# One hybrid decoder layer on one core: sample attention in 42 joined steps, forget rows a pair ahead, key pages in 2-KB runs, and three smaller edits

## The chip, the core and the metric

The kernel runs on one core of a Trainium2 chip. A core has five engines that each run their own queue of instructions in order: TensorE (PE, matrix products), VectorE (DVE), ScalarE (ACT), GpSimd (POOL) and SyncE (SP, which here only issues transfers and loads registers), and 16 DMA engines that carry the transfers which SP and ACT issue. Engines wait for one another by semaphores. The metric is the device time of one execution in microseconds; lower is better.

## The reference

One step of a decoder layer with three mixers side by side, in float32, for 1024 prompt tokens and for 8 samples of 8 new tokens each, all with the same weights:

```python
hn = rmsnorm(x, norm_pre)
u_a, z_a, q, k, v, f_lin, z_b, z_c, xbc, dt_raw, gates = split_cols(hn @ w_in)
y_a = pool_mixer(u_a) * silu(z_a)                        # A
o_b = fox_prompt(q, k, v, logf) or fox_sample(q, k, v, logf, past pages of k, v, logf)
y_b = o_b * silu(z_b)                                    # B
y_c = gated_group_rmsnorm(ssd_scan(conv(xbc), dt), z_c)  # C
g = sigmoid(gates)
m = g[0] * (y_a @ w_branch_a) + g[1] * (y_b @ w_branch_b) + g[2] * (y_c @ w_branch_c)
out = x + rmsnorm(m @ w_out, norm_post)
```

For a sample, attention runs over 1024 past positions, which lie in 8 pages of 128 positions (8 heads x 64) that a page table names, and over the 8 new ones. A logit is the product of query and key plus the difference of cumulated log-forget terms.

## The kernel before, in words

The 1088 tokens (NT) stand in columns, cut into chunks of 384, 384 and 320. Products need float32 accuracy, so each is done as three products of rounded operands: a matrix is split into a high part (`wh`, `hh`, `yh`, `ch`, `woh`, a cast on ACT) and the rest (`wl`, `hl`, `yl`, `cl`, `wol`, a subtraction on DVE or POOL), and `mm3` multiplies high by high, high by low and low by high.

The stages, in order: the projections and mixers A, B (prompt) and C; then the sample stage; then the A and B branches; the C branch; the output projection. The gate projections (`g<-hh,wh` and so on, from `gate_steps`) need only `hn`, so they are cut into steps and laid between the steps of other stages: `interleave(main, n_main, side, n_side, lag)` takes a step of the main work, then as many gate steps as are due by count; the lag keeps gate work from being scheduled earlier than the main step so many steps back.

The sample stage (`samples`, lines 896 to 1040) goes through four pairs m of samples. `load_k` and `load_v` bring pages by SP: it loads a page number into a register (`TENSOR_LOAD`, `ptab`), then issues the transfer of 256 KB (`kr<-ck`, two pages to a tile; `vr<-cv`, one). `scores(m)` fills three PSUM tiles s0, s1, s2 with products of the queries (`QB`, 32 columns at a time) with the K tiles and the new keys (`ksm`). `softmax(m)` loads the row of forget terms (`ck<-ckqD`), and on line 962 a DVE reduction adds it to the scores and takes the running minimum; exponentials (`T`) and normalisation follow. `values(m)` transposes the probabilities on PE (`pa<-cst,T`, `pa<-cst,Pn`), multiplies them by V pages (`po<-vr,PT`, `po<-vsm,PTn`) and stores the rows `ysm` that become the sample part of `ybD`. All PSUM tiles of this stage come from one pool of 5 buffers.

In the A/B stage (lines 1066 to 1100) the rows `yaD`, `ybD` come back by SP into a ring `fs` of three and are split into `yh` and `yl`; then for each of eight output rows 72 matmuls (`g<-yh,wh`), whose results DVE multiplies by gates that SP loads from `gD` into a ring `st` of five (`ld`); rows `ycD` are loaded, scaled and split into `ch`, `cl` between them. The C stage (lines 1101 to 1111) does the same with `ch`, `cl`. The output projection (from line 1113) loads `wo` in 16 halves into tiles `woh`, `wol` that lie over `ch`, `cl`.

## Time and profile before

| | |
|---|---|
| time, median of 3 runs | 1424.1 us (1422.5 to 1424.3) |
| the profiled execution | 1424.75 us, its span 1423.0 us |
| PE busy | 1374.1 us, 97% of the span |
| DVE, ACT, POOL busy | 47%, 36%, 31% |
| granted TensorE clock, mean | 0.992 of full speed |
| moved by DMA | 213.80 MB, 150 GB/s over the span |

The span is the time from the first to the last instruction of that execution. Busy times of different engines overlap. A matmul's row lasts longer than the distance to the next one, since matmuls are pipelined; what one costs is read from start to start. The clock has two levels, 1.2 and 2.4 GHz; a share below 1.00 in a stretch says that part of the stretch ran at the lower one.

### The profile page before, as it was taken

To read this page: it belongs to the slowest core of one execution; us is meant where nothing else is said; L and a number is where in the kernel's file an instruction comes from. 1 tells how busy PE (TensorE), PEld (TensorE's weight loads), DVE (VectorE), ACT (ScalarE), POOL (GpSimd) and SP (SyncE) were. 2 spreads that over 40 slices of the span, in tenths; PEclk is the share of its full clock that TensorE was granted. 3 is DMA by queue.
4 is the path that set the end of the run, shared out by engine and by line. 5 is a ranking of instruction groups with operands and counts; after the bars stand their busy time and mean duration, and the time that the engine had idled before them with its cause. 6 is when DMAs were issued, how large, how long until landed. Compare 5 with 4: busy or idle time off the path is not lost.

```text
span 1423.0 us, 23680 instructions
## 1 busy us (share of the span) xinstructions
PE 1374.1 (97%) x8936; PEld 1277.4 (90%) x8936; DVE 671.5 (47%) x1315; ACT 514.4 (36%) x1108; POOL 435.9 (31%) x383
## 2 busy tenths in 40 slices
PE   6999999999999999999999999998999999999997
PEld 5989999999999999998799898776789989999786
DVE  7493448536725833765963863110111663333423
ACT  6221255345534534546535642121123321122311
POOL 3124322222222222223644544111111353454300
PEclk9999999999999999999999999999899999999999
DMA  6124311411321241138675755988765985532421
GB/s 216 52 75 128 110 54 62 144 60 47 108 82 54 77 129 54 46 116 275 198 237 183 228 191 179 279 255 264 228 231 189 299 293 186 170 123 76 159 86 66
DMA packets 145471, 213.80 MB, mean 150 GB/s; under 512 B 20604, under 2 KB 78926, under 8 KB 145358
## 3 DMA queue, kind: packets, MB, share of 16 engines
q1 hardware_dynamic: 116878, 151.21, 33.4%
q10 hardware_dynamic: 28224, 60.83, 13.0%
q8 instruction: 70, 1.15, 0.3%
q0 software_dynamic: 256, 0.26, 0.1%
q14 instruction: 43, 0.35, 0.1%
HBM read 159.79 MB, written 54.58 MB: 151 GB/s over the span
## 4 chain that ended last, share of the span: by engine, by line
PE 82%; DMA 6%; DVE 6%; issue 2%; SPq 2%; ACT 1%; POOL 1%; DVEq 0%; ACTq 0%; POOLq 0%
PE g L71 60%; PE o L71 7%; PE po L71 4%; PE pa L71 4%; PE pa L75 3%; DMA kr<-ck 1%; PE pi L71 1%; DMA E<-cuD 1%; PE ph L71 1%; PE py L71 1%; PE s L71 1%; DMA fs<-ycD 1%; DVE win L449 1%; SPq L100 1%; DMA ybD<-o 1%
## 5 line engine op out<-in xcount | busy, mean ns | idle before, releaser
L71 PE MATMUL g<-hh,wh 128*128 128x384 f32 (+1 forms) x1632 | 545.9, 336 | 2.4 <-DVE z L237 1.5
L71 PE MATMUL g<-hh,wl 128*128 128x384 f32 (+1 forms) x1632 | 539.3, 331 | 0.0
L71 PE MATMUL g<-hl,wh 128*128 128x384 f32 (+1 forms) x1632 | 536.8, 329 | 0.3 <-DVE hl L303 0.3
L177 POOL TENSOR_TENSOR wl<-raw,wh 128x512 fp32r<-128x512 f32 x168 | 233.5, 1391 | 592.2 <-ACT wh L176 447.8
L71 PEld LDWEIGHTS g<-hh,wh 128*128 128x128 f32 x1632 | 308.1, 189 | 21.6 <-issue 14.3
L71 PEld LDWEIGHTS g<-hl,wh 128*128 128x128 f32 x1632 | 308.3, 189 | 4.9 <-issue 2.1
L71 PEld LDWEIGHTS g<-hh,wl 128*128 128x128 f32 x1632 | 308.0, 189 | 3.6 <-issue 1.6
L176 ACT CAST wh<-raw 128x512 fp32r<-128x512 f32 x168 | 103.9, 619 | 341.6 <-PE g L71 318.0
L599 POOL TENSOR_TENSOR ckd<-ckb,cst 128x128 f32<-128x128 f32 x64 | 33.3, 527 | 118.3 <-DVE mn L613 98.9
L71 PE MATMUL g<-yh,wh 128*128 128x384 f32 (+1 forms) x192 | 63.8, 332 | 5.0 <-DVE ld L1088 5.0
L249 ACT ACTIVATE gt<-g 128x384 f32<-128x384 f32 (+1 forms) x72 | 33.6, 470 | 88.1 <-PE g L71 63.2
L639 ACT CAST Ph<-pa 128x512 fp32r<-128x512 f32 (+1 forms) x96 | 44.7, 480 | 56.2 <-PE pa L75 51.9
L640 DVE TENSOR_TENSOR Pl<-pa,Ph 128x512 fp32r<-128x512 f32 (+1 forms) x96 | 51.3, 553 | 26.7 <-ACT Ph L639 20.2
L71 PE MATMUL g<-yh,wl 128*128 128x384 f32 (+1 forms) x192 | 63.6, 331 | 0.0
L71 PE MATMUL g<-yl,wh 128*128 128x384 f32 (+1 forms) x192 | 63.5, 331 | 0.0
L71 PE MATMUL g<-ch,wl 128*128 128x384 f32 (+1 forms) x192 | 62.7, 327 | 0.0
L71 PE MATMUL g<-cl,wh 128*128 128x384 f32 (+1 forms) x192 | 62.6, 326 | 0.0
L71 PE MATMUL g<-ch,wh 128*128 128x384 f32 (+1 forms) x192 | 62.6, 326 | 0.0
L617 ACT ACTIVATE T<-T,mn 128x128 f32<-128x128 f32 (+3 forms) x64 | 49.7, 777 | 30.8 <-DVE mn L613 30.8
L718 ACT ACTIVATE E<-E,cumN 128x128 f32<-128x128 f32 (+1 forms) x144 | 43.5, 383 | 37.9 <-DMA E<-cuD 31.3
L75 PE MATMUL pa<-cst,T 128*128 128x128 f32 x320 | 53.1, 272 | 0.0
L71 PE MATMUL o<-wol,mh 128*128 128x512 f32 x128 | 50.1, 399 | 0.9 <-DVE wol L1123 0.9
(266 smaller groups left out, 2057.6 us busy)
## 6 DMA issues: line engine op xcount, KB each, us to landing
raw<-w ACTq DMA_DIRECT2D x164, 256.0 KB
kr<-ck SPq DMA_DIRECT2D x64, 256.0 KB
vr<-cv SPq DMA_DIRECT2D x64, 256.0 KB
gD<-gt ACTq DMA_DIRECT2D x24, 544.0 KB
ld<-gD SPq DMA_DIRECT2D x24, 544.0 KB
E<-cuD SPq DMA_DIRECT2D x16, 512.0 KB
mD<-ld SPq DMA_DIRECT2D x8, 544.0 KB
fs<-mD SPq DMA_DIRECT2D x8, 544.0 KB
```

What stands on the lines that cost most here:

```text
L71: last["pe"] = nc.tensor.matmul(**kw)
L75: last["pe"] = nc.tensor.transpose(*args)
L100: recent.append(SP.dma_start(out=out, in_=in_))
L176: S.copy(wh, raw)
L177: G.tensor_tensor(wl, raw, wh.bitcast(F), op=SUB)
L249: S.activation(gt[:, a:b], ps, AF.Tanh, scale=0.5)
L449: V.tensor_tensor(dst[:, 2 * w - 1:W], src[:, 2 * w - 1:W], src[:, w - 1:W - w], op=ADD)
L599: G.tensor_tensor(ckd, ckb[e][:, i * 128:n], cst[:, C_M30:C_M30 + 128], op=ADD)
L617: S.activation(T[:, 0:n], T[:, 0:n], AF.Exp, scale=-1.0, bias=cur, accum_out=l[:, e, i:i + 1])
L639: S.copy(Ph[:, q0:512], ps[:, q0:512])
L640: V.tensor_tensor(Pl[:, q0:512], ps[:, q0:512], Ph[:, q0:512].bitcast(F), op=SUB)
L718: S.activation(E[0:nt, h, 0:nt], E[0:nt, h, 0:nt], AF.Relu, scale=-1.0, bias=cumN[0:nt, c, r0 + h:r0 + h + 1])
```

## The change

1. `samples` has 42 steps instead of 92: a scores step is now a K tile of each sample of the pair, a values step four V pages instead of two, and several steps of different kinds are taken together; the last step of a pair's values is taken with the first of the next pair's (`late`). The lag is 12 steps instead of 30.
2. The load of the forget row `ck` and the addition to its last columns stand at the start of `scores(m)` instead of at that of `softmax(m)`.
3. A K tile is laid out by page, so that a page's transfer writes 2 KB in one run to each partition instead of four runs of 512 B; the score products read two runs of 128 columns. The rings hold 8 K tiles and 10 V pages instead of 6 and 8; 6 K tiles and 8 V pages are asked for ahead instead of 5 and 7.
4. For odd rows k POOL computes `yl` instead of DVE.
5. `wo`'s first k-tile has two tiles of its own, `wo0h` and `wo0l`, from the ring `st`, loaded ahead of the C stage. The products of that k-tile for the first two row blocks are written ahead of the rest.

```diff
@@ -23 +23 @@
-LAG = (99, 99, 40, 30)
+LAG = (99, 99, 40, 12)
@@ -899,2 +899,2 @@
-        ak = px.enter_context(tc.tile_pool(name="ak", bufs=6))
-        av = px.enter_context(tc.tile_pool(name="av", bufs=8))
+        ak = px.enter_context(tc.tile_pool(name="ak", bufs=8))
+        av = px.enter_context(tc.tile_pool(name="av", bufs=10))
@@ -916 +916 @@
-                        kr = ak.tile([128, 4, 256], F, tag="kr", name="kr")
+                        kr = ak.tile([128, 2, 4, 128], F, tag="kr", name="kr")
@@ -918 +918 @@
-                            page_dma(out=kr[:, :, p * 128:p * 128 + 128],
+                            page_dma(out=kr[:, p],
@@ -920 +920 @@
-                        kraw.append(kr)
+                        kraw.append(kr.rearrange("p u c s -> p c u s"))
@@ -934 +934,5 @@
-            pss = score[m] = [psa(f"s{n}") for n in range(3)]
+            ck = a2.tile([128, 1032], F, tag="ck", name="ck")
+            SP.dma_start(out=ck, in_=ckqD[16 * m:16 * m + 16].rearrange("r q s -> (r q) s"))
+            V.tensor_tensor(ck[:, 1024:1032], ck[:, 1024:1032], cst[:, C_CA8:C_CA8 + 8], op=ADD)
+            pss = [psa(f"s{n}") for n in range(3)]
+            score[m] = pss, ck
@@ -944 +947,0 @@
-            yield
@@ -948,2 +951,2 @@
-                    products(pss[u // 2][:, u % 2 * 256:u % 2 * 256 + 256], bb, kraw.pop(0))
-                    yield
+                    products(pss[u // 2][:, u % 2 * 256:u % 2 * 256 + 256].rearrange("p (u s) -> p u s", u=2), bb, kraw.pop(0))
+                yield
@@ -953,4 +956 @@
-            pss, pn = score.pop(m), Pn[m % 2]
-            ck = a2.tile([128, 1032], F, tag="ck", name="ck")
-            SP.dma_start(out=ck, in_=ckqD[16 * m:16 * m + 16].rearrange("r q s -> (r q) s"))
-            V.tensor_tensor(ck[:, 1024:1032], ck[:, 1024:1032], cst[:, C_CA8:C_CA8 + 8], op=ADD)
+            (pss, ck), pn = score.pop(m), Pn[m % 2]
@@ -1005 +1005 @@
-                    if p % 2:
+                    if p % 4 == 3:
@@ -1027 +1027 @@
-            for _ in range(7):
+            for _ in range(8):
@@ -1029,0 +1030 @@
+            late = iter(())
@@ -1034,2 +1035,2 @@
-                for x in (s, v, s, v, s, v, k, v, k, v, k, v, k, v, k, v, k, v, k, v, k, v, k, v):
-                    if next(x, "end") != "end":
+                for x in ((s, late, v), (s,), (s,), (v, k), (v, k), (v, k), (v, k), (v,)):
+                    if [1 for g in x if next(g, "end") != "end"]:
@@ -1036,0 +1038,3 @@
+                late = v
+            next(late)
+            yield
@@ -1042 +1046 @@
-        for _ in range(5):
+        for _ in range(6):
@@ -1044 +1048 @@
-        interleave(samples(), 92, gate_steps(SHARE[2]), 6 * SHARE[2], LAG[3])
+        interleave(samples(), 42, gate_steps(SHARE[2]), 6 * SHARE[2], LAG[3])
@@ -1071 +1075 @@
-        V.tensor_tensor(yl[:, k], t, yh[:, k].bitcast(F), op=SUB)
+        (G if k % 2 else V).tensor_tensor(yl[:, k], t, yh[:, k].bitcast(F), op=SUB)
@@ -1100,0 +1105,13 @@
+    def load_wo(k, wh, wl):
+
+        for n in range(2):
+            sl = slice(n * 512, n * 512 + 512)
+            raw = wr.tile([128, 512], F, tag="raw", name="raw")
+            SP.dma_start(out=raw, in_=d["wo"][k, :, sl])
+            S.copy(wh[:, sl], raw)
+            (G if n else V).tensor_tensor(wl[:, sl], raw, wh[:, sl].bitcast(F), op=SUB)
+
+
+    wo = [[stq.tile([128, 1024], R, tag="st", name=x) for x in ("wo0h", "wo0l")]]
+    load_wo(0, *wo[0])
+
@@ -1118,7 +1135,3 @@
-    for k in range(8):
-        for n in range(2):
-            raw = wr.tile([128, 512], F, tag="raw", name="raw")
-            SP.dma_start(out=raw, in_=d["wo"][k, :, n * 512:n * 512 + 512])
-            S.copy(wh[:, k, n * 512:n * 512 + 512], raw)
-            (G if n else V).tensor_tensor(wl[:, k, n * 512:n * 512 + 512], raw,
-                                          wh[:, k, n * 512:n * 512 + 512].bitcast(F), op=SUB)
+    for k in range(1, 8):
+        wo.append([wh[:, k], wl[:, k]])
+        load_wo(k, *wo[k])
@@ -1129,0 +1143,15 @@
+    def out_mm(po, i, n, ks):
+        sl, tt = slice(n * 512, n * 512 + 512), slice(i * 128, i * 128 + 128)
+        for k in ks:
+            wh, wl = (x[:, sl] for x in wo[k])
+            if i < 8:
+                mm3(po, mh[:, k, tt], ml[:, k, tt], wh, wl, k == 0, k == 7)
+            else:
+                two = [(128, wh), (64, wl)]
+                for m_, x in two if k < 7 else two[::-1]:
+                    PE.matmul(out=po[0:m_], lhsT=mt[k // 4][:, k % 4, 0:m_], rhs=x,
+                              start=(k == 0 and m_ == 128), stop=(k == 7 and m_ == 128))
+
+    begun = {(i, n): psa(f"o{n}") for i in range(2) for n in range(2)}
+    for (i, n), po in begun.items():
+        out_mm(po, i, n, [0])
@@ -1140,9 +1168,5 @@
-            po = psa(f"o{n}")
-            for k in range(8):
-                if i < 8:
-                    mm3(po, mh[:, k, tt], ml[:, k, tt], wh[:, k, sl], wl[:, k, sl], k == 0, k == 7)
-                else:
-                    two = [(128, wh), (64, wl)]
-                    for m_, x in two if k < 7 else two[::-1]:
-                        PE.matmul(out=po[0:m_], lhsT=mt[k // 4][:, k % 4, 0:m_], rhs=x[:, k, sl],
-                                  start=(k == 0 and m_ == 128), stop=(k == 7 and m_ == 128))
+            po = begun.pop((i, n), None)
+            if po is None:
+                po = psa(f"o{n}")
+                out_mm(po, i, n, [0])
+            out_mm(po, i, n, range(1, 8))
```

What the change moves in the order of instructions is shown at three places. First SP, where it issues the rows `ck`. Before, the third of the four rows in the program (`ck_11178`, for the third pair; `ptab` is the page table, `ISA` an arithmetic instruction on registers):

```order
L100 DMA kr_11125<-ck 128x4x128
L955 DMA ck_11178<-ckqD_154 128x1032
L97 TENSOR_LOAD ptab_84
L97 ISA x2
L100 ISA
L100 DMA vr_11230<-cv 128x512
```

Now the third row:

```order
L97 TENSOR_LOAD ptab_84
L97 ISA x2
L935 DMA ck_10655<-ckqD_154 128x1032
L100 ISA
L100 DMA vr_10625<-cv 128x512
```

and the first two, with the first K page (`rst` is a small tile of the C mixer, `rsD1` where it is stored):

```order
L812 DMA ycD1_142<-gch_9399 512x1x64
L935 DMA ck_9698<-ckqD_154 128x1032
L848 DMA rsD1_160<-rst_9440 9x128
L935 DMA ck_10181<-ckqD_154 128x1032
L100 ISA
L100 DMA kr_9572<-ck 128x512
```

The third row stood right behind a run of K pages, with V pages after it; now 54 pages stand ahead of it, 44 of K and 10 of V. The rows of the first and the second pair stand ahead of all pages, with the store of `rst` between them.

PE, before, where the first value products come (`po<-vr,PT`):

```order
L71 MATMUL g<-hl,wh 128x384
L71 MATMUL g<-hh,wl 128x384
L75 MATMUL pa<-cst,Pn_9477 128x128
L71 MATMUL g<-hh,wh 128x384
L71 MATMUL g<-hl,wh 128x384
L71 MATMUL g<-hh,wl 128x384
L71 MATMUL po<-vr,PT 32x128 x8
L71 MATMUL g<-hh,wh 128x320
```

and now:

```order
L71 MATMUL g<-hh,wl 128x384
L71 MATMUL g<-hh,wh 128x384
L71 MATMUL g<-hl,wh 128x384
L71 MATMUL g<-hh,wl 128x384
L71 MATMUL po<-vr,PT 32x128 x16
L71 MATMUL s_10660<-ksm,QB 32x8 x8
L71 MATMUL s_10658<-kr,QB 32x256 x8
```

A values step has twice as many products, and the products of new keys and of two K tiles of a later pair (`s_10660`, `s_10658`) stand right behind it without gate matmuls between. Over the whole stage, from the first `ksm` product to the first matmul with `yh`, 58 runs of gate matmuls, 896 in all, become 36 runs with the same 896.

POOL at the end of the sample stage, before:

```order
L177 TENSOR_TENSOR wl_12599<-raw_12596,wh_12598 128x512
L177 TENSOR_TENSOR wl_12605<-raw_12602,wh_12604 128x512
L177 TENSOR_TENSOR wl_12691<-raw_12688,wh_12690 128x512
L177 TENSOR_TENSOR wl_12697<-raw_12694,wh_12696 128x512
L177 TENSOR_TENSOR wl_12830<-raw_12827,wh_12829 128x512
L177 TENSOR_TENSOR wl_12836<-raw_12833,wh_12835 128x512
```

and now:

```order
L177 TENSOR_TENSOR wl_12605<-raw_12602,wh_12604 128x512
L1075 TENSOR_TENSOR yl_12783<-fs_12788,yh_12782 128x1088
L177 TENSOR_TENSOR wl_12691<-raw_12688,wh_12690 128x512
L1075 TENSOR_TENSOR yl_12783<-fs_12796,yh_12782 128x1088
L177 TENSOR_TENSOR wl_12697<-raw_12694,wh_12696 128x512
L1075 TENSOR_TENSOR yl_12783<-fs_12804,yh_12782 128x1088
L177 TENSOR_TENSOR wl_12830<-raw_12827,wh_12829 128x512
L1075 TENSOR_TENSOR yl_12783<-fs_12812,yh_12782 128x1088
L177 TENSOR_TENSOR wl_12836<-raw_12833,wh_12835 128x512
```

The four `yl` subtractions of odd rows now stand between the weight splits `wl`, the last (from `fs_12812`) is behind `wl_12830`. On PE 168 gate matmuls instead of 156 stand between the last transposes of the sample stage and the first matmul with `yh`, and the output projection begins with 15 products of `wo0h` and `wo0l`.

## Rows read from the trace of the kernel before

**Rows 1.** The page's first part: busy time of each engine, its share of the span, and instructions.

```profile
PE 1374.1 (97%) x8936; PEld 1277.4 (90%) x8936; DVE 671.5 (47%) x1315; ACT 514.4 (36%) x1108; POOL 435.9 (31%) x383
```

**Rows 2.** Busy time of each engine in stretches of 100 us. Columns: stretch, its length, then busy us with the number of instructions for PE, weight loads, DVE, ACT and POOL, then the granted TensorE clock, the busy share of the DMA engines and GB/s.

```profile
900.00:1000.00 100.00, 85.55 (x742) 70.01 (x743) 9.76 (x32) 16.32 (x32) 12.38 (x10) 0.95 0.83 260
1000.00:1100.00 100.00, 100.00 (x975) 87.81 (x975) 12.59 (x38) 24.44 (x46) 15.61 (x12) 0.98 0.66 216
1100.00:1200.00 100.00, 95.00 (x562) 93.93 (x562) 54.10 (x67) 25.72 (x35) 43.60 (x26) 0.98 0.82 269
```

**Rows 3.** The list of waits of PE over the whole span. Columns: engine and line that waited, what it waited for, us in total, times, longest.

```profile
PE pa L75 <- DVE mn L962: 10.2, 1, 10.2
PE g L71 <- DVE ld L1088: 5.0, 3, 1.9
PE s L71 <- DMA kr<-ck: 4.3, 3, 2.7
```

**Rows 4.** The timeline around the longest of these waits, in this order: PE's transpose of `Pn` into `pa`, DVE's addition to the row `ck` ahead of its reductions, and SP's issues of six K pages and of the `ck` load. Columns: start, duration, engine and line (q: issued by the engine's queue), operation, out<-in, shape, count, and in brackets the idle time before it and what ended it.

```profile
999.41 0.47 PE L75 MATMUL pa<-cst,Pn 128*128 128x128 f32 x1 [10.20 <-DVE mn L962]
...
998.48 0.17 DVE L956 TENSOR_TENSOR ck<-ck,cst 128x8 f32<-128x8 f32 x1 [15.41 <-DMA ck<-ckqD]
...
984.76 8.20 SPq L100 DMA_DIRECT2D kr<-ck  x6
993.06 0.56 SPq L955 DMA_DIRECT2D ck<-ckqD  x1
```

**Rows 5.** Stretches of 10 us, columns as in rows 2; the third column from the end is the granted clock, as a share of full speed.

```profile
900.00:910.00 10.00, 7.32 (x75) 5.55 (x79) 0.78 (x3) 0.98 (x2) 0.83 (x1) 1.00 0.65 214
910.00:920.00 10.00, 9.81 (x72) 8.08 (x73) 2.28 (x8) 2.09 (x4) 1.29 (x1) 0.83 1.05 298
...
1000.00:1010.00 10.00, 10.00 (x92) 8.87 (x95) 3.06 (x10) 3.38 (x7) 1.27 (x1) 0.80 0.39 112
...
1310.00:1320.00 10.00, 8.42 (x41) 7.29 (x40) 6.44 (x7) 4.12 (x9) 6.21 (x5) 0.90 0.08 27
1320.00:1330.00 10.00, 10.00 (x41) 7.96 (x41) 3.19 (x5) 4.34 (x8) 3.40 (x3) 0.93 0.64 211
```

**Rows 6.** PE's timeline at the first K products of the sample stage. `s<-kr,QB` are score products, four instructions (eight records) for a K tile of two pages.

```profile
899.99 2.37 PE L71 MATMUL s<-kr,QB 128*32 128x256 f32 x40
902.28 0.44 PE L71 MATMUL g<-hl,wh 128*128 128x384 f32 x1
...
909.93 0.64 PE L71 MATMUL s<-kr,QB 128*32 128x256 f32 x8 [2.68 <-DMA kr<-ck]
910.50 0.41 PE L71 MATMUL g<-hh,wh 128*128 128x320 f32 x1
```

**Rows 7.** PE's timeline where value products `po` alternate with a run of twelve gate matmuls: a product, the first, second and last matmul of the run, the next product.

```profile
1080.68 0.65 PE L71 MATMUL po<-vr,PT 128*32 128x128 f32 x16
1081.26 0.44 PE L71 MATMUL g<-hh,wh 128*128 128x384 f32 x1
1081.54 0.34 PE L71 MATMUL g<-hl,wh 128*128 128x384 f32 x1
...
1083.28 0.34 PE L71 MATMUL g<-hh,wl 128*128 128x384 f32 x1
1083.54 0.64 PE L71 MATMUL po<-vr,PT 128*32 128x128 f32 x16
```

**Rows 8.** The page stream. First the instructions that issue K and V pages (line, engine, operation, tile, count, shortest/median/longest duration in ns, first and last start); then the page queue in two stretches, 930 to 947 (mostly K pages) and 1060 to 1080 (V pages): packets, MB moved, share of the 16 DMA engines' time; then SP's first K issues, the copy into `rst` on ACT, and SP's store of `rst`.

```profile
L100 SPq DMA_DIRECT2D kr<-ck x64: 542/544/2028, 885.2 to 1021.7; - x64
...
L100 SPq DMA_DIRECT2D vr<-cv x64: 332/333/1379, 918.5 to 1081.4; - x64
...
q1 hardware_dynamic: 6296, 3.13, 64.2%
...
q1 hardware_dynamic: 1619, 2.93, 42.8%
...
885.17 10.72 SPq L100 DMA_DIRECT2D kr<-ck  x12
...
895.66 0.25 ACT L847 COPY rst<-pa 9x128 f32<-9x128 f32 x1 [1.98 <-DMA kr<-ck]
...
899.44 0.35 SPq L848 DMA_DIRECT2D rsD<-rst  x1
```

**Rows 9.** The end of the sample stage: the first matmul with `yh`, the first three `yl` subtractions and the last on DVE, SP's issue of `gD` loads, and the first matmul of PE that waits for one. Last, the subtractions of the same size that POOL does in this stage (count, shortest/median/longest ns).

```profile
1117.47 0.34 PE L71 MATMUL g<-yh,wh 128*128 128x384 f32 x1
...
1097.27 3.70 DVE L1071 TENSOR_TENSOR yl<-fs,yh 128x1088 fp32r<-128x1088 f32 x3 [4.30 <-ACT yh L1070]
1114.59 1.29 DVE L1071 TENSOR_TENSOR yl<-fs,yh 128x1088 fp32r<-128x1088 f32 x1 [2.86 <-ACT yh L1070]
...
1117.64 1.85 SPq L1063 DMA_DIRECT2D ld<-gD  x4
...
1125.48 0.44 PE L71 MATMUL g<-yh,wh 128*128 128x384 f32 x1 [1.92 <-DVE ld L1088]
...
L1099 POOL TENSOR_TENSOR cl<-fs,ch x4: 2539/2748/3615, 1122.8 to 1159.1; 128x1088 fp32r<-128x1088 f32 x4
```

**Rows 10.** PE's timeline at the start of the output projection.

```profile
1315.65 0.49 PE L71 MATMUL o<-woh,mh 128*128 128x512 f32 x1 [0.71 <-ACT woh L1122]
1317.02 0.50 PE L71 MATMUL o<-wol,mh 128*128 128x512 f32 x1 [0.87 <-DVE wol L1123]
```

## The prediction

> **What bounds the kernel now.** I read the busy times first, then TensorE (PE) by windows of 100 us, then its list of waits, then the timeline around each wait. PE is busy for 1374.1 us of the span [rows 1]: it sets the end, and an edit pays only if it shortens PE's own work, removes a PE wait, or gives PE its clock back. The windows show where there is something to remove: 14.5 us idle in 900 to 1000 and 5.0 in 1100 to 1200 [rows 2]; 1000 to 1100 is full. The list of waits names them: one of 10.2 us behind a VectorE (DVE) reduction of line 962, three for K pages (4.3 us), three of 5.0 us in the A/B branch stage [rows 3]; two at the start of the output projection make 1.6 us [rows 10].
>
> The long one can be followed back. At 999.41 the transpose into `pa` got its PSUM buffer. It waited for a reduction of line 962, which needs the row `ck`; DVE had idled 15.41 us for it until 998.48; and SyncE (SP) issued that load at 993.06, behind six K pages whose issues, each with its register load, took 984.76 to 992.96 [rows 4]. So the load was late in SP's order, not slow.
>
> An idle PE also loses clock. In 910 to 920, after a K wait, the granted clock is 0.83; in 1000 to 1010 it is 0.80; in 1310 to 1330 it is 0.90 and 0.93 [rows 5]. Ten us at 0.83 instead of 1.00 are 1.7 us of lost work; so the dips cost 1.7, 2.0 and 1.7 us beside the waits.
>
> **The change part by part.**
>
> *Joined steps.* Counted in PE's program order from the first `ksm` product to the first `gy` matmul, 58 runs of gate matmuls become 36, with the same 896 gate matmuls and the same products. What does a switch cost? Ten steps inside a run take 1.74 us, 0.174 each; from the last gate to the product 0.26, and from the first gate after it to the second 0.28 [rows 7]: 0.19 us above 0.174 twice over, so about 0.20 per switch pair. Splitting K products costs a little more: 40 records take 2.29 us (0.057 each, 0.46 for 8), eight alone 0.57 [rows 6]. So 0.20 to 0.31 per pair; 22 fewer give -4.4 to -6.8. I take **-6**.
>
> *The `ck` row a pair ahead.* In the new order of SP the third row's load stands behind 54 pages: at 0.97 us a page from 897 (both below) it is issued at 949 and there by 955, as it took 5.4 us in before (993.06 to 998.48). PE reaches the transposes whose buffer hangs on its reductions at about 972, after V page 15 (964, below) and 36 more gate matmuls. The 10.2 us go, and the dip after them: 10.2 + 2.0 = **-12.2**. At 1.15 us a page the row comes at 964, still ahead; so I exclude that much of it stays.
>
> *K pages of 2-KB runs, two more ahead, wider rings.* K waits of 4.3 us and the dip of 1.7 can go: -6.0. What does a page cost? SP spends 0.544 us issuing a K page and 0.333 a V page, which already has 2-KB runs; in 930 to 947, mostly K pages, the queue moved 3.13 MB in 64.2% of 17 us, 287 GB/s; in 1060 to 1080, V pages, 2.93 MB in 42.8% of 20 us, 342 GB/s [rows 8]. A page is 262 KB: 0.91 and 0.77 us. With about a fifth of the DMA engines on the other queue (an estimate from both windows) that is 1.15 and 0.97 us per page.
>
> But the stream starts later and PE comes sooner. In before twelve K pages were issued from 885.17. Now the wider K ring lies over `rst`, so the first page must wait until the store `rsD<-rst` lands. That store was issued at 899.44; its source was copied at 895.66, after an idle time for a K page's DMA lane that is not yet in use now [rows 8]. I put the first page at 897 (894 to 900). PE needs few pages early: the new order has 33 gate matmuls ahead of the first K tile where before had five tiles at once at 899.99. The tight place is V pages 12 to 15, the 61st to 64th page transfers. PE gets there after 272 gate matmuls (by 0.165, mixed widths: 45), 22 K tiles (10), 12 V pages (3.4), small products and transposes (2.5) and 18 switches (3.6): 899.6 + 64.5 = 964. The pages get there at 897 + 64 x 0.97 + 2.5 for the row and the landing = 961.6, or, were a page no cheaper than before, at 973. So a new wait of 0 to 9 us, with a dip of up to 2. Nearest are the V rows, whose layout the K pages now have: **+1.5** (0 to +11).
>
> By the Trainium skill (DMA: Bandwidth & Descriptors, Specifications) a transfer is at line rate from 512 B up, so runs of 512 B would have nothing to gain; by that rule the wait would be the 9 us and the dip. The trace does not agree: 287 against 342 GB/s at equal engine share.
>
> *`yl` of odd rows on GpSimd (POOL).* The rows pass through a ring of three: row 4 is loaded when the `yl` of row 1 is done, row 7 after that of row 4; when the last has released its buffer, SP goes on to the `ycD` rows and then, from 1117.64, to four `gD` loads, on whose first arrival PE waits until 1125.48, 1.92 us [rows 9]. The first three `yl` take 3.70 us on DVE, the last one 1.29 [rows 9]. Now rows 1 and 7 of this chain are POOL's, where a subtraction of this size has a median of 2.748 us [rows 9]: each ends some 1.5 us later, 2.9 together. POOL has weight splits between, but the one ahead of the last `yl` is due much earlier. Cover: the gates after the last values product are 168 instead of 156, 12 x 0.165 = 2 us more. Net **+1**; -1 if rows of even k, no longer behind odd ones on DVE, make the chain shorter, +4 if nothing covers and POOL takes its longest, 3.615 us.
>
> *First output k-tile apart.* At 1315.65 and 1317.02 PE waited 0.71 and 0.87 us for the cast and split of `wo`, since their tiles lie over `ch`/`cl`, which the last branch matmuls read [rows 10]. Now 15 matmuls of k = 0 with tiles made long before come first; at 0.232 us (0.174 by 512/384 columns) they are 3.5 us, more than the 2.1 us from the end of the branch (1315.65 - 0.71 = 1314.94) to 1317.02. Waits and dip go: -1.6 - 1.7 = -3.3; two ring buffers fewer for `gD` in the C stage could take some of it. **-3** (-1.5 to -3.3).
>
> **The sum**: -6 - 12.2 - 6 + 1.5 + 1 - 3 = -24.7. The profiled execution took 1424.75 us, so 1400.05; the median of the runs is 0.65 lower: 1399.4, so **1399** in round numbers.
>
> **The rivals.**
>
> *The pages come too late* (17%). In before the 10.2-us stall also let the page stream catch up; without it PE runs into V pages 12 to 15, or into K pages right at the start if the first page goes out at 900. Nine us and a dip of 2 in place of 1.5: 1399 + 9.5 = 1408.5; half of it, 1404. For: DMA share is 0.83 already in 900 to 1000 [rows 2]. Against: 342 GB/s in V's rows.
>
> *Given back in the A/B stage* (13%). Its three waits of 5.0 us are for `gD`, loaded by SP behind the branch rows. POOL has four subtractions more there, and one late row delays all loads behind it; 4 us and a dip of 2 in place of 1 give 1399 + 5 = 1404, and if the later two waits also grow by 2 each, 1408.
>
> *More than I count* (8%). No page wait at all, POOL's chain hidden, switches at 0.31: 1399 - 1.5 - 1 - 0.8 = 1395.7, and a few us less if the other small dips of 900 to 1100 go too.
>
> *Slower: joined bursts cost the clock* (4%, and 3% for a draw). The new order has 16 values steps of 4 pages, eight of them joined with scores into some 2.3 us of nothing but 32-row products, in which most of the array is idle. If the clock fell after each of the 16, as after the stalls (1.7 to 2.0 us), that would be 27 to 32 us against a gain of 24.7: 1399 + 27 = 1426 to 1431. It decides from 1.5 us a burst. Against it: 899.99 to 902.28 is such a burst of 40 records, and the window 900 to 910 has a granted clock of 1.00 even with a wait in it [rows 5, 6]. The Trainium skill (TensorE: Matmul & The Clock Gate, A second HAM failure mode) tells of short idles between groups of matmuls that bring the clock down; by that rule bursts would count, and this trace agrees only for true waits.
>
> *The change does nothing where it says*: if the third `ck` still comes behind pages, 12.2 us stay: 1411; the order of SP speaks against it (2%).
>
> **How the numbers follow.** My forecast has 53%, with its own range of 1394 to 1404. The range of **1391 to 1409** takes in late pages and the A/B stage at their bounds; about 15% lie outside, most of it above. A change of 0.2% (2.8 us) is about what can be told from none here: faster 0.93, same 0.03, slower 0.04.
>
> **What would show it.** Right: no PE wait on line 962's reductions in 990 to 1000; clock 1.00 in 1000 to 1010 of before; K issues of about 0.33 us; the first `gy` matmul, at 1117.47 before [rows 9], 22.7 us earlier, near 1095; the first output matmul without a wait. Wrong: a PE wait on `vr` near 964 or on `kr` near 905 to 945; a longer wait on `ld` after the first `gy` run; a clock below 1.00 behind bursts without a wait.

## The result, and the profile after

The changed kernel takes 1408.8 us (median of 4 runs, 1407.01 to 1410.02), the kernel before 1424.2 beside it; the ratio is 0.9896, with a 95% interval of [0.9877, 0.9914]. So it is faster, by 15 us where 25 were forecast; 0.9896 of the 1424.1 that the forecast started from are 1409.3, just beyond the upper end of its range. The profiled execution took 1407.01 us, its span is 1405.2.

Where the time went by stage (from the first such matmul on PE to the first of the next kind; the last ends with the span; us):

| stage | before | after | difference | forecast |
|---|---|---|---|---|
| up to the first score product | 899.55 | 899.98 | +0.4 | 0 |
| sample stage, to the first matmul with `yh` | 217.9 | 204.7 | -13.3 | -22.7 |
| A/B, to the first with `ch` | 102.3 | 100.0 | -2.3 | +1 |
| C and output projection | 203.3 | 200.7 | -2.6 | -3 |

So the sample stage lacks 9.4 us of its forecast; the A/B stage gives 3.3 more than forecast. From PE's list of waits over the whole span, columns as in [rows 3]:

```profile
PE po L71 <- DMA vr<-cv: 8.1, 9, 3.6
PE g L71 <- DVE ld L1092: 4.3, 3, 2.8
PE o L71 <- ACT woh L1111: 0.2, 1, 0.2
```

The wait on line 962 and those on K pages are gone. In their place there are 8.1 us for V pages, which the kernel before didn't have. The timeline of PE where the most of it lies:

```profile
962.61 0.43 PE L71 MATMUL po<-vr,PT 128*32 128x128 f32 x8 [1.22 <-DMA vr<-cv]
963.28 0.43 PE L71 MATMUL po<-vr,PT 128*32 128x128 f32 x8 [0.24 <-DMA vr<-cv]
963.52 1.05 PE L71 MATMUL s<-kr,QB 128*32 128x256 f32 x16
...
970.44 0.43 PE L71 MATMUL po<-vr,PT 128*32 128x128 f32 x8 [3.59 <-DMA vr<-cv]
971.76 0.43 PE L71 MATMUL po<-vr,PT 128*32 128x128 f32 x8 [0.89 <-DMA vr<-cv]
972.44 1.41 PE L71 MATMUL po<-vr,PT 128*32 128x128 f32 x16 [0.25 <-DMA vr<-cv]
```

These are V pages 10 to 15, counted from 0, eight records to a page; 12 to 15 are the 61st to 64th page transfers. Page 12 is there 3.6 us after PE is, and PE then waits for 13 and 14 as well. The 10-us windows around it (columns as in [rows 5]):

```profile
950.00:960.00 10.00, 10.00 (x156) 8.33 (x155) 0.00 (x0) 1.83 (x4) 0.83 (x2) 1.00 0.83 247
960.00:970.00 10.00, 5.39 (x65) 3.70 (x63) 0.78 (x3) 0.00 (x0) 0.63 (x1) 1.00 0.93 331
970.00:980.00 10.00, 8.30 (x82) 6.17 (x83) 2.70 (x7) 2.26 (x5) 1.17 (x1) 0.83 0.78 232
```

PE falls to 5.39 us of 10, and the granted clock behind it is 0.83: another 1.7 us (a fall of the clock behind a wait is called a dip here). The rest of what the change promised is there: in 950 to 960, full of joined bursts, the clock is 1.00, and the output projection begins without the two waits of [rows 10]:

```profile
1299.47 0.31 PE L71 MATMUL g<-ch,wl 128*128 128x320 f32 x1
1299.62 0.39 PE L71 MATMUL o<-wo0h,mh 128*128 128x512 f32 x1
1299.85 0.39 PE L71 MATMUL o<-wo0l,mh 128*128 128x512 f32 x1
```

From one matmul to the next it is 0.15 us across the border of the stages, where [rows 10] had a wait of 0.71 and one of 0.87. Two of 0.2 us each come later.

Why the V pages are late is in SP's issues of pages:

```profile
894.85 0.44 SPq L848 DMA_DIRECT2D rsD<-rst  x1
...
899.22 24.98 SPq L100 DMA_DIRECT2D kr<-ck  x28
924.98 9.27 SPq L100 DMA_DIRECT2D vr<-cv  x8
935.09 18.47 SPq L100 DMA_DIRECT2D kr<-ck  x16
954.33 2.24 SPq L100 DMA_DIRECT2D vr<-cv  x2
...
964.59 4.67 SPq L100 DMA_DIRECT2D vr<-cv  x4
```

The first K page goes out at 899.22, 4.4 us after the store of `rst` that it waits for. The first 24 need (918.62 - 899.22)/23 = 0.84 us each, faster than the 0.97 I had put. But from the 25th on it is slower: eight V pages in 9.27 us, sixteen K pages in 18.47, so 1.21 to 1.28 from one to the next (the last one's 0.33 us taken off), although each issue takes 0.333 us:

```profile
L100 SPq DMA_DIRECT2D kr<-ck x64: 332/333/791, 899.2 to 1003.8; - x64
```
```profile
L97 SPq TENSOR_LOAD <-ptab x65: 263/269/1158, 919.0 to 998.9; - x65
```

What fills the space is the register load of the page's number, from 919.0 on: 65 of them between 919.0 and 998.9, each with its arithmetic behind it. SP waits for nothing else there; its list of waits from 919 to 970 has one line:

```profile
SPq L100 <- PE g L71: 0.4, 1, 0.4
```

### The profile page after: what moved, and what is told of

Read it like the earlier page. It is cut to its first block, busy times and chain, and to the rows that moved or that the text cites. A ratio compares the mean times of both kernels' runs of the same rounds, so it can differ in the third digit from the quotient of the medians.

```text
span 1405.2 us, 23690 instructions
## 1 busy us (share of the span) xinstructions
PE 1363.5 (97%) x8936; PEld 1271.9 (91%) x8936; DVE 671.1 (48%) x1311; ACT 515.5 (37%) x1108; POOL 447.8 (32%) x387
## 4 chain that ended last, share of the span: by engine, by line
PE 80%; DVE 7%; DMA 5%; issue 2%; SPq 2%; POOL 2%; ACT 2%; ACTq 0%; DVEq 0%; POOLq 0%
PE g L71 59%; PE o L71 6%; PE pa L71 4%; PE pa L75 4%; PE po L71 3%; PE pi L71 1%; PE ph L71 1%; PE s L71 1%; DMA vr<-cv 1%; PE py L71 1%; POOL wl L177 1%; DVE win L449 1%; SPq L100 1%; SPq L97 1%; DMA ybD<-o 1%
## 5 line engine op out<-in xcount | busy, mean ns | idle before, releaser
L513 DVE SCALAR_TENSOR_TENSOR cacc<-xp,parh,cacc 128x1112 f32<-128x1112 f32 x36 | 50.8, 1410 | 0.4
```

The lines of the kernel that those rows point to most:

```text
L513: V.scalar_tensor_tensor(acc[:, 0:1112], xp[:, x:x + 1112], w[x], acc[:, 0:1112], op0=MUL, op1=ADD)
```

## The experiments

Three theories for the late V pages stood against each other: SP's own pace (its register loads), the DMA engines' rate, and the late first page. Then the parts of the change were undone one by one, and again with the cause removed. Page times are read from SP's timeline; the stage is the sample stage, 217.9 us before and 204.7 after. Some edits also change the order in which PE gets its work; it is given as the number of runs of gate matmuls in the stage, counted as in the section on the change (58 before, 36 after).

### Registers 48 transfers ahead (e1)

```diff
-            if len(recent) >= 24:
-                st.enter_context(tc.issue_after(recent[-24].ins))
+            if len(recent) >= 48:
+                st.enter_context(tc.issue_after(recent[-48].ins))
```

> The changed kernel with one number altered: page numbers may be loaded into registers 48 page transfers ahead instead of 24, so that most register loads leave the space between two page issues. Theory 1 (SyncE's own issue pace makes the V pages late: 1.11 to 1.17 us from one page to the next from the 25th page on, against 0.51 to 0.56 without a register load): PE's waits on vr, 8.1 us in the changed kernel, fall below 3 us, the dip of 1.7 us behind them goes, and the time falls by 5 to 9 us, to 1400 to 1404. Theory 2 (the DMA engines are full anyway, share 0.9 to 1.0 from 900 to 930): the pages still come at 0.9 to 1.0 us each, waits of 4 to 7 us stay, and the time falls by less than 3 us. Theory 3 (the late first page, 899.22, is what counts): no change.

Ratio 0.992 [0.989, 0.995]: not faster than the change, against the first two theories as I had put them; by the time alone it is what the third had. The profile says why. PE's waits, and SP's timeline:

```profile
PE g L71 <- ACT gt L249: 5.2, 3, 2.5
PE po L71 <- DMA vr<-cv: 5.0, 8, 1.3
```
```profile
921.72 5.76 SPq L100 DMA_DIRECT2D vr<-cv  x8
927.92 14.40 SPq L100 DMA_DIRECT2D kr<-ck  x16
942.50 0.85 SPq L100 DMA_DIRECT2D vr<-cv  x2
944.03 0.33 SPq L935 DMA_DIRECT2D ck<-ckqD  x1
959.94 0.92 SPq L100 DMA_DIRECT2D vr<-cv  x2
```
```profile
L97 SPq TENSOR_LOAD <-ptab x26: 262/264/1061, 943.4 to 959.2; - x26
```

Without loads between, 24 pages from the 29th to the 52nd go out in 20.8 us (921.72 to 942.50), 0.87 each, where the changed kernel needed 1.2: so the pace was SP's. But the loads had only been moved. 26 of them stand in one batch from 943.4 to 959.2, 0.6 us each, in front of V page 10, and page 61 goes out at 963.4, hardly earlier than 964.6. And the faster stream stopped ACT:

```profile
943.47 0.33 ACTq L173 DMA_DIRECT2D raw<-w  x1
943.86 0.87 ACT L249 ACTIVATE gt<-g 128x384 f32<-128x384 f32 x2 [6.54 <-DMA kr<-ck]
```

ACT had waited 6.54 us for a K page's DMA, as the row names it: in this kernel the transfers of SP and ACT share eight completion semaphores by turns, and the one for ACT's next transfer (`raw<-w` at 943.47) was still with a K page. PE waited 2.18 us at 944.40 for the gate eviction behind it. At 985.40 the same happens with a V page (ACT waits 8.53 us, PE 2.47); those two are most of the 5.2 us.

### A ring of 6 K tiles (e2)

```diff
-        ak = px.enter_context(tc.tile_pool(name="ak", bufs=8))
+        ak = px.enter_context(tc.tile_pool(name="ak", bufs=6))
```

> The changed kernel with the ring of K tiles back at 6, so that it no longer lies over the tile whose store the first K page waited for; K pages can start near 885 as in the kernel before, twelve of them ahead of the first product. Theory 3 (late start): 14 us of lead for the page stream, waits on vr fall from 8.1 to below 3 us, time 1400 to 1404. Theory 1 (issue pace): the twelve pages are a gain of 12 x 0.9 = 11 us at the start, but a ring of 6 holds the stream back later; the waits fall by 2 to 5 us, time 1404 to 1407. Against both: a ring of 6 brings waits on K pages of 2 to 4 us, as before.

Ratio 0.9894 [0.9864, 0.9924], no difference to 0.9896 that could be told. The first page goes out at 884.93, 14 us earlier, but the 61st at 958.6, only 6 earlier; 5.7 us of waits on V pages stay, 0.8 on K pages come. The late first page is a part of the cause and not the larger one. The edit isn't clean, though: PE's order has 28 runs of gate matmuls with a ring of 6, and in this execution the clock falls further in the windows from 960 and from 1000 (0.83, 0.81, 0.85), 5.1 us where the change lost 1.7.

### Both (e3)

> Both at once: registers 48 transfers ahead and a ring of 6 K tiles. If pace and start both matter, neither waits on kr nor on vr stay (below 1 us in all), the granted clock is 1.00 from 900 to 1100, and the time is 1397 to 1400, which is what was forecast for the change. If the DMA engines are the limit, 1402 to 1406.

Ratio 0.9866 [0.9836, 0.9896]. The waits on V pages are 1.7 us, on K pages 2.0, and one of 3.7 on ACT has come, with the same kind of blocked transfer. The time, 1403.5 us, is that of the second expectation, but not for its reason: the pages are less late, and ACT is still held up.

### K pages in runs of 512 B again (e4)

```diff
-                        kr = ak.tile([128, 2, 4, 128], F, tag="kr", name="kr")
+                        kr = ak.tile([128, 4, 256], F, tag="kr", name="kr")
-                            page_dma(out=kr[:, p],
+                            page_dma(out=kr[:, :, p * 128:p * 128 + 128],
...
-                        kraw.append(kr.rearrange("p u c s -> p c u s"))
+                        kraw.append(kr)
...
```

> The changed kernel with K tiles laid out as before, so a page goes to a partition in four runs of 512 B. If 2-KB runs are worth what the rows of before said (0.91 against 0.77 us of DMA time, 0.54 against 0.33 us of issue), 60 pages ahead of the critical V pages are 8 to 12 us later: waits on vr and kr of 14 to 20 us and a time of 1415 to 1421. If transfers are at line rate from 512 B on, only the issue time counts, 0.2 us a page: 1410 to 1412.

Ratio 0.9965 [0.995, 0.998]: 9.8 us slower than the change (0.0069 of 1424). The time, 1416.6 us, is that of the first theory, but the waits on pages are 10.9 us where it had 14 to 20, and PE's order has 44 runs of gate matmuls instead of 36, which can account for some 2 us (an estimate, 8 at the 0.29 us of e14 below). The 61st page goes out at 972.6. Whether it is the rate or only the issue could not be told here; e15 tells.

### The 92 steps again (e5)

```diff
-LAG = (99, 99, 40, 12)
+LAG = (99, 99, 40, 30)
...
-                    if p % 4 == 3:
+                    if p % 2:
...
-                for x in ((s, late, v), (s,), (s,), (v, k), (v, k), (v, k), (v, k), (v,)):
-                    if [1 for g in x if next(g, "end") != "end"]:
+                for x in (s, v, s, v, s, v, k, v, k, v, k, v, k, v, k, v, k, v, k, v, k, v, k, v):
+                    if next(x, "end") != "end":
...
-        interleave(samples(), 42, gate_steps(SHARE[2]), 6 * SHARE[2], LAG[3])
+        interleave(samples(), 92, gate_steps(SHARE[2]), 6 * SHARE[2], LAG[3])
```

> The changed kernel with the 92 separate steps and the lag of 30 put back, everything else as changed. Forecast's theory: 22 switches more cost 4.4 to 6.8 us, so a ratio to before of 0.993 to 0.995 instead of 0.9896. Rival: PE only arrives later at V pages that were late anyway, so the waits on vr (8.1 us) shrink by what the switches cost and the ratio stays within 0.002 of 0.9896.

Ratio 0.989 [0.9858, 0.9922], the same as with joined steps: the rival, by the time. There is no wait on any page in its list, and PE is full in the window where the change lost 6.3 us:

```profile
900.00:1000.00 100.00, 99.97 (x913) 81.00 (x912) 11.06 (x41) 20.53 (x40) 14.85 (x12) 1.00 0.90 299
```

So what joining gave, V pages took. But the rival's reason isn't the whole one, since SP's order has changed too:

```profile
952.08 3.76 SPq L100 DMA_DIRECT2D vr<-cv  x4
...
957.15 1.49 SPq L100 DMA_DIRECT2D vr<-cv  x2
...
961.68 1.48 SPq L100 DMA_DIRECT2D vr<-cv  x2
```

With separate steps K and V pages alternate by twos there, so V pages 12 and 13 are the 57th and 58th transfers and not the 61st and 62nd. Page 12 goes out 57.8 us after the stage's first score product instead of 64.6, and PE reaches it at 63.9, not later than in the change (66.9, after 1.5 us of waits). Pages 14 and 15 are now the 61st and 62nd, and PE asks for them only at 69.3. So joining also asks for these four V pages at one point and puts them further back in SP's queue.

### The forget row late again (e6), and early alone (e12)

```diff
-            ck = a2.tile([128, 1032], F, tag="ck", name="ck")
-            SP.dma_start(out=ck, in_=ckqD[16 * m:16 * m + 16].rearrange("r q s -> (r q) s"))
-            V.tensor_tensor(ck[:, 1024:1032], ck[:, 1024:1032], cst[:, C_CA8:C_CA8 + 8], op=ADD)
             pss = [psa(f"s{n}") for n in range(3)]
...
         def softmax(m):
...
+            ck = a2.tile([128, 1032], F, tag="ck", name="ck")
+            SP.dma_start(out=ck, in_=ckqD[16 * m:16 * m + 16].rearrange("r q s -> (r q) s"))
+            V.tensor_tensor(ck[:, 1024:1032], ck[:, 1024:1032], cst[:, C_CA8:C_CA8 + 8], op=ADD)
```

> The changed kernel with the load of the forget row put back to the start of softmax. Forecast's theory: a stall of 8 to 12 us on line 962's reductions comes back with its dip, ratio 0.996 to 0.999. Rival: a stall there gives the page stream time, so part of the waits on vr goes in exchange, and only 3 to 7 us are lost: ratio 0.992 to 0.9945. Second rival: with wider rings and joined steps the row is in time even from softmax, ratio unchanged.

e6 has a ratio of 0.9917 [0.9889, 0.9946]. A stall on line 962's reductions is back at half its size, and the waits on V pages have halved: the exchange of the first rival, for 3 us in all. The interval overlaps that of the change.

```profile
PE s L71 <- DVE mn L962: 5.5, 1, 5.5
PE po L71 <- DMA vr<-cv: 3.9, 3, 2.4
```

e12 is the kernel before with the opposite edit, the row moved to `scores`, and nothing else.

> The kernel before with one part of the change alone: the forget row loaded a pair ahead. Forecast's theory: the stall of 10.2 us and its dip of 2 go, ratio 0.9905 to 0.9925. Rival: the stall was also the time in which pages caught up, so waits on vr or kr take 3 to 7 us of it back: ratio 0.993 to 0.997.

Ratio 0.992 [0.9891, 0.9948]: 11.4 us of 1424, the forecast's theory, where its term was 12.2. The waits on pages stay what they were, with one more of 1.2:

```profile
PE s L71 <- DMA kr<-ck: 4.5, 3, 2.7
PE po L71 <- DMA vr<-cv: 1.2, 1, 1.2
```

So this part alone makes three quarters of what the whole change measures (the intervals overlap widely).

### POOL's share of `yl` (e7) and the first k-tile (e8) undone

```diff
-        (G if k % 2 else V).tensor_tensor(yl[:, k], t, yh[:, k].bitcast(F), op=SUB)
+        V.tensor_tensor(yl[:, k], t, yh[:, k].bitcast(F), op=SUB)
```

> The changed kernel with all yl subtractions on VectorE. Forecast's theory: POOL's share lengthens the chain to the first gD load by 2.9 us, so PE's first wait on ld in the A/B stage falls from 2.8 to below 1 us and the time by 1 to 2.5 us. Rival: the chain ends at the gD transfers, which other loads hold up, and the wait stays at 2 to 3 us, time within 0.5 us.

Ratio 0.9893 [0.9864, 0.9922], no difference. The first wait on `ld` is 0.58 us there, as the forecast's theory had it, but a second of 1.04 follows, and e11 and e16 below don't repeat it. For e8 `wo`'s first k-tile is loaded with the rest, as before:

```diff
-    wo = [[stq.tile([128, 1024], R, tag="st", name=x) for x in ("wo0h", "wo0l")]]
-    load_wo(0, *wo[0])
+    wo = []
...
-    for k in range(1, 8):
+    for k in range(8):
...
-    begun = {(i, n): psa(f"o{n}") for i in range(2) for n in range(2)}
-    for (i, n), po in begun.items():
-        out_mm(po, i, n, [0])
...
-            po = begun.pop((i, n), None)
-            if po is None:
-                po = psa(f"o{n}")
-                out_mm(po, i, n, [0])
-            out_mm(po, i, n, range(1, 8))
+            po = psa(f"o{n}")
+            out_mm(po, i, n, range(8))
```

> The changed kernel with the first k-tile of wo loaded with the others, after the C stage. Forecast's theory: the two waits of 1.6 us and a dip of 1.7 come back at the start of the output projection, 3 us, ratio about 0.9917. Rival: the dip doesn't come back, 1.2 to 1.6 us.

Ratio 0.9923 [0.9897, 0.995], 0.0027 or 3.8 us above the change, with intervals that overlap. The two waits are back, 0.71 and 0.88 us and a third of 0.34, and the clock from 1290 to 1330 is 1.00: the waits came back, the dip did not, in the execution that was profiled. There the last two stages take 202.7 us, 2.0 more than with the change.

### One register load for a K page and its V page (e9)

```diff
-    recent = []
-    def page(b, p):
+    held, free = {}, []
+    def page(b, p, keep):
+        if keep is False:
+            return held.pop((b, p))
         with ExitStack() as st:
-            if len(recent) >= 24:
-                st.enter_context(tc.issue_after(recent[-24].ins))
-            return SP.value_load(ptab[0:1, b * 8 + p:b * 8 + p + 1], min_val=0, max_val=79)
+            n = len(free) + len(held) - 40
+            if n >= 0:
...
+                st.enter_context(tc.issue_after(free[n].ins))
+            held[b, p] = SP.value_load(ptab[0:1, b * 8 + p:b * 8 + p + 1], min_val=0, max_val=79)
+        return held[b, p]
...
```

K pages call it with True, V pages with False; `free` lists the V transfers, after which a register is free again.

> The changed kernel in which a V page is addressed by the register that its K page has loaded, so SyncE makes 64 register loads instead of 128, and hardly one between two page issues. Theory 1 (SyncE's pace of 1.1 us a page, half of it the register load, makes V pages 12 to 15 late): the 61st page is issued by 957 instead of 964.6, waits on vr fall from 8.1 to below 2 us, and no wait on ACT takes their place; ratio 0.984 to 0.987. Theory 2 (8 transfers in flight and the DMA engines' rate bound the stream): the pace settles at 0.85 to 0.95 us a page, ACT's own transfers queue behind pages, and PE waits for ACT's gate evictions instead, as with 48 registers ahead; ratio 0.988 to 0.992.

Ratio 0.9834 [0.9808, 0.986], 1398.65 us: theory 1. PE's list of waits has none on a page. SP's timeline, where `kr` and `vr` now go out of line 105:

```profile
902.62 21.54 SPq L105 DMA_DIRECT2D kr<-ck  x28
924.50 5.73 SPq L105 DMA_DIRECT2D vr<-cv  x8
930.68 9.00 SPq L105 DMA_DIRECT2D kr<-ck  x12
...
958.46 3.06 SPq L105 DMA_DIRECT2D vr<-cv  x4
```
```profile
L101 SPq TENSOR_LOAD <-ptab x24: 261/268/483, 935.7 to 982.8; - x24
```

24 register loads in this stretch instead of 65; eight V pages take 5.73 us where they took 9.27. This execution began the stage 3.4 us later (the first score product at 903.39), and counted from there the 61st page goes out at 55.1 us instead of 64.6. The stage takes 194.1 us, 1.1 less than the 195.2 that the forecast had (217.9 - 22.7), with a granted clock of 1.00 from end to end. One wait on ACT of 0.8 us has come, far from what e1 had. What SP waits for has changed with it; from its list, 900 to 1000:

```profile
SPq L105 <- PE po L71: 15.4, 7, 5.8
SPq L105 <- DMA kr<-ck: 8.2, 19, 1.0
```

So now the V ring (buffers that PE has not read yet) and the transfers themselves hold the stream, at 0.84 us a page from the 29th to the 53rd, and the DMA engines are full (share 1.02 from 900 to 950). The edit does two things, fewer loads and loads further ahead; the second alone, e1, gained nothing.

### With a ring of 6 as well (e10, e13), and the parts undone on top of it (e11, e14 to e16)

> As the one before with a ring of 6 K tiles, so that K pages start near 885. Theory 1: a lead of 14 us more, no waits on kr or vr at all and ratio 0.983 to 0.985. Theory 2: the lead is used up by ring waits; waits on kr of 1 to 2 us, ratio as without it, within 0.002.

> Shared registers and a ring of 6 K tiles once more, in more rounds, beside the two kernels below. Expected ratio to before 0.979 to 0.983, no wait on kr or vr.

Ratio 0.9806 [0.9771, 0.9841] and, in more executions, 0.9813 [0.979, 0.9837]: 1392.4 and 1395.5 us, the lowest here together with e16, though the intervals overlap that of e9. e10 has no wait on a page, as its first theory had it; e13 has 0.7 us on K pages, where none was expected, and its stage takes 191.3 us. Not all of that is the earlier start: PE's order has 28 runs of gate matmuls with this ring, and 35 in e9. On top of e13, with the edit of e5:

> Shared registers and ring of 6, with the 92 separate steps and the lag of 30 put back. If joining is worth its switches once pages are in time (forecast: 4.4 to 6.8 us), this is slower than the one before by 0.003 to 0.005. Rival: joining is worth nothing, because separate steps spread the score products' reads of pages and PE waits less in later stages: within 0.0015.

Ratio 0.9881 [0.9861, 0.9901]. Neither has waits on V pages now, and joining, with its lag, is worth 0.0068 of the time, more than either theory had. The stage takes 198.8 us instead of 191.3. PE's order has 54 runs of gate matmuls instead of 28, so these are 7.5 us for 26 switches: 0.29 each. Another 3.2 us of the profiled difference lie in the A/B stage, which the edit doesn't touch. With the edit of e4:

> Shared registers and ring of 6, with K pages in four runs of 512 B to a partition. SyncE now has time to spare, so what is left is the DMA engines' rate. If 512-B runs are slower there (287 against 342 GB/s in the kernel before), waits on kr or vr of 3 to 8 us come back, ratio 0.002 to 0.006 higher. If transfers are at line rate from 512 B on, no difference beyond 0.001.

Ratio 0.9856 [0.9835, 0.9877], 0.0043 or 6 us above e13 (the intervals just touch), with 4.7 us of waits on K pages, and with e13's 28 runs. The page queue's row from 900 to 930, first e13, then e15:

```profile
q1 hardware_dynamic: 4098, 7.95, 73.8%
```
```profile
q1 hardware_dynamic: 10533, 8.03, 88.7%
```

Almost the same bytes take 73.8% of the engines' 30 us with 2-KB runs (359 GB/s at full share) and 88.7% with 512-B runs (302). With ACT's queue, which takes 13.1%, the engines are full in e15: the runs count there, and not only in SP's issues. The other two put `yl` back to VectorE, on top of e9 and of e13:

> Shared registers, and all yl subtractions on VectorE. If POOL's share of yl lengthens the chain to gD (forecast: 2.9 us, less 2 us of cover), the first wait on ld shrinks by 1 to 2.5 us and the ratio by 0.001 to 0.002 against the run with shared registers alone; if not, no difference.

> Shared registers and ring of 6, with all yl subtractions on VectorE. Forecast's theory (POOL's share of yl costs 1 us net, -1 to +4): ratio lower by 0.0005 to 0.002. Rival: the even rows no longer behind odd ones make up for it: no difference, or higher by up to 0.001.

0.9828 [0.9785, 0.9871] against 0.9834, and 0.9803 [0.9782, 0.9823] against 0.9813: no difference that these runs can tell. The first wait on `ld` is 2.85 us in e11 against 0.26 in e9, and 2.98 in e16 against 2.30 in e13; with e7's 0.58 against 2.80 it does not follow `yl`.

## Why the prediction was wrong, step by step

**What bounds it**: right. PE sets the end, and the windows and waits named the places.

**Joined steps, -6**: the mechanism holds and the size is right (0.29 us a switch by e14, where 0.20 to 0.31 was forecast; 22 of them make 6.4). The sum was wrong to count it as a gain of this kernel by itself: by e5 it is worth nothing as long as SP's pace is what it is, since PE comes earlier to V pages that stand later in SP's queue.

**The forget row, -12.2**: right. 11.4 us by e12 (7 to 16 by its interval), and no wait on line 962 after. The third row went out at 957.81 and not at 949, by the page price that is wrong below, and was still in time.

**K pages and rings, -6 and +1.5**: this is the step that failed, in its price of 0.97 us a page. The K waits and their dip went, as said. The "tight place" was the right place, V pages 12 to 15, and PE came to it when I had said (966.85 after a wait of 1.5 us, against 964). But the pages were to be there at 961.6, "897 + 64 x 0.97", and the 64th was issued at 968.9. The 0.97 was the DMA engines' time alone. From the 25th page on SP needs 1.24 us a page ((964.59 - 918.62)/37), for a register load stands before each issue: the lead of 24 loads is used up. The price stood in [rows 4], where six K pages, "each with its register load", take 8.20 us: I read them as an explanation and didn't carry them into the sum. From start to start they are (8.20 - 0.54)/5 = 1.53 us each; less 0.21 us of issue that the 2-KB runs save, 1.32. By the Trainium skill (DMA: Bandwidth & Descriptors, Latency and other measured facts) a register load has a floor of about 600 ns. The batch of e1 comes near it if the arithmetic behind each load is counted in, 26 loads in 15.8 us; the rows of the load instruction alone have a median of 0.26 us. The first page was 2.2 us later than I put it, and the first 24 pages 3 us faster than I had counted. In all the term was +9.8 (8.1 of waits and 1.7 of dip) and not +1.5, inside the bounds of 0 to +11 but near their upper end, and that is 8.3 of the 9.4 us that the stage lacks. With the loads halved (e9) the waits are gone and the stage takes what was forecast. The rival "the pages come too late", with 1408.5 us, is what happened; I had given it 17% and argued against it from the rate in V's rows, which was not the limit.

**The rule on 512 B** (the Trainium skill, DMA: Bandwidth & Descriptors, Specifications): the trace goes against it by the same fifth as in the kernel before, 359 against 302 GB/s, and with SP out of the way 512-B runs cost 6 us (e13, e15).

**`yl` on POOL, +1**: no effect can be told (e7, e11, e16), and my chain was not the one that counted. The last `yl` is POOL's, but it ends about as early before the first matmul with `yh` as it did before, and the `gD` loads go out sooner. What PE waits for is DVE, which takes the gates only after a subtraction for `cl`:

```profile
1100.23 2.53 POOL L1075 TENSOR_TENSOR yl<-fs,yh 128x1088 fp32r<-128x1088 f32 x1
```
```profile
1103.83 2.45 SPq L1067 DMA_DIRECT2D ld<-gD  x4
```
```profile
1109.25 3.64 DVE L1103 TENSOR_TENSOR cl<-fs,ch 128x1088 fp32r<-128x1088 f32 x1
1112.92 0.55 DVE L1092 SCALAR_TENSOR_TENSOR ld<-ld,g 128x384 f32<-128x384 f32 x1
```
```profile
1113.53 0.44 PE L71 MATMUL g<-yh,wh 128*128 128x384 f32 x1 [2.80 <-DVE ld L1092]
```

1102.76 is 1.9 us ahead of the stage's first matmul (1104.63), where [rows 9] had 1115.88, 1.6 ahead of 1117.47. From the issue of `gD` to PE's matmul it is 9.7 us now and was 7.8. The transfer is not what has grown: it has landed by 1111.14, 7.3 us after its issue, where it took 7.1 before (1117.64 to 1124.77). DVE is at its `cl` subtraction until 1112.89, and that is 1.7 of PE's 2.80 us. That the A/B stage is 2.3 us shorter all the same comes from its waits (4.3 after 5.0) and from its clock: 1.00 in 1100 to 1200, where [rows 2] had 0.98. It isn't shown to be a gain of the change: in e12, whose edit doesn't touch that stage, it takes 100.5 us. The 3.3 us by which it beats the forecast are luck.

**First k-tile apart, -3**: right in its waits, 1.9 us by e8; the dip of 1.7 is gone too, but it did not come back in e8's profile, so that half isn't shown. The stages give -2.6, and e8's time 3.8, with an interval too wide to say more.

**Bursts cost the clock**: fell. The joined bursts of 950 to 960 run at 1.00, and in e9 and e13 the whole stage does.

The sum with the one term replaced is -24.7 + 8.3 = -16.4, against -17.7 in the profiled execution and -15.4 of the medians. It comes this near with the help of the A/B stage.

## What to carry to other kernels

Price a stream of transfers by each thing that it passes, the engines that move it, the ring that takes it and the queue that issues it, and take the slowest: here the issuing queue was the limit, 1.24 us a page with a register load before each, and not the bandwidth, which allowed 0.84 (e9). A gain on the critical engine is worth nothing as long as the next thing it waits for keeps its own time, so what comes next has to be timed against the new, earlier arrival, and in the new order: joining steps moved the late pages back in their queue. And work that is only moved ahead can come back as a batch in front of another transfer (e1); work that is dropped, as the second register load of the same page number (e9), doesn't.

## What the runs showed that was not expected

- A stream of pages that runs far ahead stops the other queue that issues transfers: in e1 ACT waited 6.54 us for the end of a K page's transfer before its own and 8.53 us for a V page's, and PE 2.18 and 2.47 us for ACT behind them.
- Not every wait of PE costs clock. After 2.80 us of waiting at 1113.53 in the changed kernel the next matmuls come at full pace (1113.81, 1113.98: 0.17 apart), while in the kernel before the 1.92 us at 1125.48 lie in a window granted 0.85 (third column from the end; first before, then after). The forecast's price of 1.7 to 2.0 us a dip holds where a dip comes; which waits bring one these runs don't tell.

```profile
1120.00:1130.00 10.00, 8.08 (x41) 7.71 (x40) 8.78 (x9) 3.09 (x4) 6.38 (x3) 0.85 0.99 344
```
```profile
1110.00:1120.00 10.00, 7.20 (x44) 6.82 (x44) 8.05 (x9) 1.40 (x3) 5.03 (x3) 1.00 0.95 327
```
